# Turning the residual in blocks of 32 on VectorE and by small DMAs on POOL's queue

## The chip, the cores and the metric

The kernel runs on one core of one Trainium2 chip. The metric is the time of one execution on the device in microseconds (us). The profiler names the engines PE (TensorE, matmuls), PEld (its weight loads), DVE (VectorE), ACT (ScalarE), POOL (GpSimd) and SP (SyncE); SP, ACT and POOL can each issue DMAs on a queue of their own.

## What is computed

One layer of a decoder trunk over 512 tokens of width 1024, in float32. Cut to what matters here:

```
h   = rms_norm(x) ; z = h @ W_in                 # projections, gating, latent attention
x   = x + merged @ W_out                         # the residual x1
up  = conv3(rms_norm(x) @ w_up)                  # 2 x 2816 columns, causal depthwise conv, width 3
x   = x + (silu(gate) * val) @ w_down
out = rms_norm(x)                                # back to token-major rows
```

The end of the layer adds to x1 and takes a mean over the 1024 features of each token, so tokens must lie on the partitions there. Up to the up-projection the features lie on the partitions. Somewhere in between the residual x1 (512 tokens x 1024 features) has to be transposed.

## The kernel before

All matmuls run on float32 operands split in a high and a low part, three matmuls for one product (`mm3`, L79 to L82): `wsplit` lets ACT cast the high part (L70) and DVE subtract for the low part (L71).

**The residual.** `x1` is eight feature blocks j of 128 features x 512 tokens, in two tiles `x1_0` and `x1_1` of the pool hp (tags d0 and d1, L560). The same two buffers held vA before. The output projection adds to it on DVE (L571).

**The up-projection and the gated FFN** (the loop `for n in range(NF)`, 22 rounds): a round multiplies two column blocks of w_up (`pup`, 24 matmuls each), scales each by the broadcast row norm `r2` when it leaves PSUM (`conv`, `z = pup * r2`, L635), runs the convolution on ACT and DVE, and writes the product into `aT`. The last of these scalings in the program is that of block 43, `z43`. In rounds 4 to 11 `x1_turn(t, hf)` turns a piece of the residual: four PE transposes of 128x128 (L649) into a PSUM bank, and an ACT copy back into the same places of x1 (L650). In rounds 12 to 17 `fill` loads the first quarter of w_down, B11, into the six tiles `R` (L608, on SP's queue).

**The down-projection** is a scheme of seven products m1, m5, m6, m4, m3, m7, m2 (L689) of half-sized matrices; each is 11 blocks of 6 matmuls, and its right side comes in six pieces g = 0 to 5 of two blocks each (the last of one). A piece of `R` is split for the current product (`w_split`, L711), and right after that a DMA on POOL's queue adds the next quarter of w_down onto it in place (L606, `accum_op=add`), so that R[g] is the sum that the next product needs. m1 multiplies by B11 itself: its first matmul needs the cast of R[0]. For m3 the tile is loaded anew instead (L608, SP). `post`, `done` and `finish` add the products to the residual, take the squares, scale and store.

**Order and buffers.** A scheduler lays down each engine's instruction order when the program is built, by program order and priorities; each engine then works strictly in its order and waits on semaphores. A pool gives tiles of one tag the same buffers; a tile without a tag takes its name as its tag, within its pool. The pools hp and fp hold one buffer for each tag. The next tile of a tag gets the buffer when every instruction that reads or writes the earlier tile is done. Of the names below, fp holds these:

```
    r2 = fp.tile([P, S], F32, name="r2")
    aT = fp.tile([P, NF, S], F32, name="aT")
    R = [fp.tile([P, (hi - lo) * S], F32, name=f"r1_{lo}") for lo, hi in steps]
```

Of the kernel before, what the change touches and what calls it, by code (L numbers as in the profile page):

```python
# [7 lines left out]
F32 = mybir.dt.float32  # L8
# [3 lines left out]
AF = mybir.ActivationFunctionType  # L12
ALU = mybir.AluOpType
AX = mybir.AxisListType

P = 128
D = 1024
S = 512
NT = S // P
KC = D // P  # L20
# [3 lines left out]
NF = DFF // P  # L24
# [18 lines left out]
def block_kernel(ctx, tc, xT, pos, w_s, w_v, w_g, w_q, w_kv, w_o, w_u, w_d,  # L43
                 ws_t, bs, vg, vb, par, cst, fnl, out):
    nc = tc.nc
    V, A, T, G, SY = nc.vector, nc.scalar, nc.tensor, nc.gpsimd, nc.sync
# [3 lines left out]
    hp = ctx.enter_context(tc.tile_pool(name="hp", bufs=1))  # L50
    ps = ctx.enter_context(tc.tile_pool(name="ps", bufs=8, space=bass.MemoryType.PSUM))

    def bank(n):
        return ps.tile([P, 512], F32, tag="ps", name=n)
# [53 lines left out]
    ident = cstt[:, CI:CI + P]  # L108
# [66 lines left out]
    cqL = [mx.tile([P, S], F32R, name=f"cqL{i}") for i in range(2)]  # L175
    ckH = mx.tile([P, S], F32R, name="ckH")
    ckL = mx.tile([P, S], F32R, name="ckL")
    vA2 = [hp.tile([P, 2 * D], F32, tag=f"d{t}", name=f"vA{t}") for t in range(2)]
    vA = [vA2[t // 2][:, (t % 2) * D:(t % 2 + 1) * D] for t in range(NT)]

    with tc.tile_pool(name="st", bufs=2) as st:

# [22 lines left out]
        for j in range(KC):  # L205
# [7 lines left out]
            lo = half * S  # L213
# [157 lines left out]
    with tc.tile_pool(name="at", bufs=1) as at:  # L371
# [119 lines left out]
        for h in range(H):  # L491
# [30 lines left out]
            if h < NT:  # L522
                t = h
# [16 lines left out]
    with tc.tile_pool(name="mg", bufs=2) as mg:  # L540
        for h in range(H):
            zb = zbs[h] if h in zbs else gate("b", 2 * H + h)
            pm = bank(f"pm{h}")
            c = slice(h * P, (h + 1) * P)
            for n in range(NT):
                T.matmul(pm[:, n * P:(n + 1) * P], lhsT=vA[n][:, c], rhs=wst[:, h], start=True, stop=True)
            t2 = mg.tile([P, S], F32, tag="t2", name=f"t2{h}")
            V.tensor_tensor(out=t2.rearrange("p (n t) -> p n t", n=NT),
                            in0=pm.rearrange("p (n t) -> p n t", n=NT),
                            in1=bsb[:, h:h + 1].to_broadcast([P, NT, P]), op=ALU.add)  # L550
            V.tensor_tensor(out=t2, in0=uT[h], in1=t2, op=ALU.mult)
            zz = mg.tile([P, S], F32, tag="zz", name=f"zz{h}")
            V.tensor_tensor(out=zz, in0=zb, in1=yB[h], op=ALU.mult)
            V.tensor_tensor(out=zz, in0=zz, in1=t2, op=ALU.add)
            mH.append(uy.tile([P, S], F32R, tag=f"u{h}", name=f"mH{h}"))
            mL.append(uy.tile([P, S], F32R, tag=f"y{h}", name=f"mL{h}"))
            split(mH[h], mL[h], zz)


        x1t = [hp.tile([P, NT, NT, P], F32, tag=f"d{t}", name=f"x1_{t}") for t in range(2)]  # L560
        x1 = [x1t[j // NT][:, j % NT].rearrange("p t c -> p (t c)") for j in range(KC)]
        acc2 = hp.tile([P, S], F32, name="acc2")
        for j in range(KC):
            SY.dma_start(x1[j], xT[j])
            raw = wtile(w_o[j], f"o{j}")
            wh, wl = wsplit(raw, f"o{j}")
            po = bank(f"pout{j}")
            for h in range(H):
                c = slice(h * P, (h + 1) * P)
                mm3(po, wh[:, c], wl[:, c], mH[h], mL[h], h == 0, h == H - 1)  # L570
            V.tensor_tensor(out=x1[j], in0=po, in1=x1[j], op=ALU.add)  # L571
            htiles(j, "f")
            g_ = part[:, PFF + j:PFF + j + 1]
            A.mul(hH[j], x1[j], g_)
            V.scalar_tensor_tensor(out=hL[j], in0=x1[j], scalar=g_, in1=hH[j].bitcast(F32),
                                   op0=ALU.mult, op1=ALU.subtract)
            sq = acc2 if j == 0 else mg.tile([P, S], F32, tag="sq2", name=f"sq2_{j}")
            A.activation(out=sq, in_=x1[j], func=AF.Square)
            if j:
                V.tensor_tensor(out=acc2, in0=acc2, in1=sq, op=ALU.add)  # L580
# [14 lines left out]
    NS = len(steps)  # L595
    B11, B12, B21, B22 = (w_d[k, f] for k in range(2) for f in range(2))

    R = [fp.tile([P, (hi - lo) * S], F32, name=f"r1_{lo}") for lo, hi in steps]

    def cols(g):  # L600
        lo, hi = steps[g]
        return slice(lo * S, hi * S)

    def fill(q, g, add=True):
        if add:
            G.dma_start(R[g], q[:, cols(g)], accum_op=ALU.add)  # L606
        else:
            SY.dma_start(R[g], q[:, cols(g)])  # L608

    def a_sides(lo, hi):  # L610

# [30 lines left out]
                               op0=ALU.mult, op1=ALU.add)  # L642
        return y

    def x1_turn(t, hf):

        pt = bank(f"pt{t}{hf}")
        for q in range(NT):
            T.transpose(pt[:, q * P:(q + 1) * P], x1t[hf][:, q, t, :], ident)  # L649
        A.copy(x1t[hf][:, :, t, :], pt.rearrange("p (q c) -> p q c", q=NT))  # L650

    with tc.tile_pool(name="f2", bufs=2) as f2:
        for n in range(NF):
            i = n // 2 + (n % 2) * KH
            pg = up(2 * n)
            if n == 0:
                rt = rooted([acc2], 0, f2, "f")
                pv = up(1)
                A.copy(r2, over_partitions(rt, f2, "f"))
            yg = conv(pg, i)  # L660
            if n:
                pv = up(2 * n + 1)
            A.activation(out=yg, in_=yg, func=AF.Silu)  # L663
            yv = conv(pv, NF + i)
            V.tensor_tensor(out=aT[:, i], in0=yg, in1=yv, op=ALU.mult)
            if n % 4 == 3 or n == NF - 1:
                a_sides(n // 4 * 2, n // 2 + 1)
            if 4 <= n < 12:
                x1_turn((n - 4) // 2, n % 2)
            if 12 <= n < 12 + NS:  # L670
                fill(B11, n - 12, False)

# [43 lines left out]

    def res(t, f):

        return x1t[f][:, :, t, :]

    def b3(t):
        return t.rearrange("p (q c) -> p q c", q=NT)

    def plus(t, f, t_):
        V.tensor_tensor(out=res(t, f), in0=res(t, f), in1=b3(t_), op=ALU.add)

    def done(t, f, p_, op=ALU.add):
        V.tensor_tensor(out=res(t, f), in0=res(t, f), in1=b3(p_), op=op)  # L730
        j_ = dp.tile([P, S], F32, tag="j", name=f"j{t}{f}", bufs=2)
        A.activation(out=b3(j_), in_=res(t, f), func=AF.Square, accum_out=ms[:, t, f:f + 1])
        if f:
            V.tensor_tensor(out=res(t, f), in0=res(t, f), in1=b3(gfb[:, S:]), op=ALU.mult)

    def finish(t):

        V.tensor_scalar(out=ms[:, t, 2:3], in0=ms[:, t, 0:1], scalar1=ms[:, t, 1:2], scalar2=1.0 / D,
                        op0=ALU.add, op1=ALU.mult)
        V.tensor_scalar(out=ms[:, t, 2:3], in0=ms[:, t, 2:3], scalar1=EPS, scalar2=None, op0=ALU.add)  # L740
        G.tensor_tensor(out=ms[:, t, 3:4], in0=ms[:, t, 2:3], in1=mhalf[:, 0:1], op=ALU.pow)
        r_ = ms[:, t, 3:4]
        V.scalar_tensor_tensor(out=res(t, 0), in0=res(t, 0), scalar=r_, in1=b3(gfb[:, :S]),
                               op0=ALU.mult, op1=ALU.mult)
        A.mul(res(t, 1), res(t, 1), r_)
        SY.dma_start(out[t, :, :S], res(t, 0))
        A.dma_start(out[t, :, S:], res(t, 1))
# [143 lines left out]
```

## Time and profile before

| | us |
|---|---|
| median of 3 runs | 696.66 (696.41 to 697.33) |
| the profiled execution, its own time | 697.01 |
| span in its trace, first to last instruction | 695.3 |
| up-projection on PE, first to last matmul | about 336 to 581 |
| down-projection on PE, first matmul | 580.75 |

The page of the profile gives for each engine the busy time and its share of the span. A row of a timeline has the start in us, the duration in us, the engine, the line, the operation with its output and input tiles (without buffer numbers), the shapes and, in square brackets, the idle time of that engine ahead of it and what ended it. "POOLq" and "SPq" are the queues on which an engine issues DMAs; a DMA's time "to landing" runs from its issue to its completion. A row of PE times one matmul with its pipeline, so starts, not durations, tell the rate.

### The profile page before, as it was taken

The numbers are of one execution on the slowest core, as the hardware profiler recorded it, in microseconds if no ns is written. First come the engines' busy times: TensorE is split into PE (matmuls) and PEld (weight loads), VectorE is DVE, ScalarE is ACT, GpSimd is POOL, SyncE is SP. The second block draws the span as 40 slices with busy tenths as digits, with TensorE's granted clock in tenths as the row PEclk, the third lists the DMA queues.
The fourth block names the chain that finished last, engine by engine and source line by source line (L and its number), as shares of the span: only waits on it lengthen the run. The fifth ranks groups of instructions, "written<-read, shape, count | busy, mean of one in ns | idle before, by whom it ended". The sixth has DMA issues, their size and how long they took to land.

```text
span 695.3 us, 8489 instructions
## 1 busy us (share of the span) xinstructions
PE 684.6 (98%) x3183; PEld 569.4 (82%) x3183; DVE 522.6 (75%) x859; ACT 353.9 (51%) x519; POOL 36.0 (5%) x42
## 2 busy tenths in 40 slices
PE   9999999999999999999999999999999999999994
PEld 6888888888888888888888888888888888888883
DVE  7966699877768678855577868778677789579884
ACT  6465556775765552343354344444344335565672
POOL 0000110000000000000100000000000002330201
PEclk9999999999999999999999999999999999999998
DMA  8424522131120112353542222223322236997824
GB/s 269 153 78 139 186 84 83 61 115 31 61 88 34 62 61 91 109 177 107 180 170 90 92 91 90 92 90 99 114 91 91 91 91 118 197 187 202 159 76 122
DMA packets 28026, 78.67 MB, mean 113 GB/s; under 512 B 3024, under 2 KB 7632, under 8 KB 27984
## 3 DMA queue, kind: packets, MB, share of 16 engines
q1 hardware_dynamic: 21408, 62.92, 27.4%
q0 software_dynamic: 3456, 11.54, 9.3%
q10 hardware_dynamic: 3120, 3.67, 1.7%
q8 instruction: 25, 0.41, 0.2%
q14 instruction: 17, 0.14, 0.1%
HBM read 76.02 MB, written 2.10 MB: 112 GB/s over the span
## 4 chain that ended last, share of the span: by engine, by line
PE 96%; DVE 1%; issue 1%; POOL 0%; ACT 0%; POOLq 0%
PE pup L80 12%; PE pup L82 12%; PE pup L81 11%; PE m L82 4%; PE m L81 4%; PE m L80 4%; PE pout L81 2%; PE pv L80 2%; PE pout L80 2%; PE pza L81 2%; PE pza L80 2%; PE pzb L80 2%; PE pzb L82 2%; PE pzu L81 2%; PE pzb L81 2%; PE pv L82 2%
## 5 line engine op out<-in xcount | busy, mean ns | idle before, releaser
L70 ACT CAST wh_u<-wr_u 128x1024 fp32r<-128x1024 f32 x44 | 46.3, 1051 | 84.4 <-issue 49.6
L71 DVE TENSOR_TENSOR wl_u<-wr_u,wh_u 128x1024 fp32r<-128x1024 f32 x44 | 53.9, 1224 | 9.9 <-ACT wh_u L70 9.6
L635 DVE TENSOR_TENSOR z<-pup,r 128x512 f32<-128x512 f32 x44 | 30.3, 690 | 40.3 <-PE pup L82 40.3
L82 PE MATMUL m<-wh_m,al_m 128*128 128x512 f32 x132 | 51.5, 390 | 0.6 <-DVE al_m L77 0.6
L80 PE MATMUL m<-wh_m,ah_m 128*128 128x512 f32 x132 | 51.4, 389 | 0.0
L81 PE MATMUL m<-wl_m,ah_m 128*128 128x512 f32 x132 | 51.4, 389 | 0.0
L70 ACT CAST wh_g<-wr_g 128x1024 fp32r<-128x1024 f32 x24 | 25.2, 1049 | 49.4 <-issue 30.6
L71 DVE TENSOR_TENSOR wl_m<-r,wh_m 128x1024 fp32r<-128x1024 f32 (+1 forms) x36 | 40.7, 1131 | 6.3 <-ACT wh_m L70 6.3
L70 ACT CAST wh_m<-r 128x1024 fp32r<-128x1024 f32 (+1 forms) x36 | 35.3, 980 | 19.6 <-PE m L82 19.1
L637 ACT ACTIVATE y<-z,part 128x512 f32<-128x512 f32 x44 | 35.7, 814 | 2.6 <-DVE z L635 2.4
L663 ACT ACTIVATE y<-y 128x512 f32<-128x512 f32 x22 | 13.9, 633 | 45.0 <-DVE y L641 45.0
L606 POOL DMA_DIRECT2D r<-in_w_d_dram x24 | 21.4, 890 | 287.0 <-DVE wl_m L71 270.7
L71 DVE TENSOR_TENSOR wl_g<-wr_g,wh_g 128x1024 fp32r<-128x1024 f32 x24 | 29.4, 1223 | 7.2 <-ACT wh_g L70 7.1
L641 DVE SCALAR_TENSOR_TENSOR y<-z,part,y 128x512 f32<-128x512 f32 x44 | 33.0, 751 | 1.4
L639 DVE SCALAR_TENSOR_TENSOR y<-z,part,y 128x512 f32<-128x512 f32 x44 | 32.8, 747 | 0.7 <-ACT y L637 0.7
L82 PEld LDWEIGHTS m<-wh_m,al_m 128*128 128x128 f32 x132 | 24.8, 188 | 6.1 <-DVE al_m L77 1.0
L81 PEld LDWEIGHTS m<-wl_m,ah_m 128*128 128x128 f32 x132 | 24.8, 188 | 5.2
L80 PEld LDWEIGHTS m<-wh_m,ah_m 128*128 128x128 f32 x132 | 24.8, 188 | 5.2
L81 PE MATMUL pout<-mL,wh_o 128*128 128x512 f32 x64 | 25.3, 395 | 0.0
L80 PE MATMUL pout<-mH,wh_o 128*128 128x512 f32 x64 | 25.0, 394 | 0.0
L82 PE MATMUL pout<-mH,wl_o 128*128 128x512 f32 x64 | 24.9, 389 | 0.0
L77 DVE TENSOR_TENSOR al_m<-aT,ah_m 128x1024 fp32r<-128x1024 f32 (+1 forms) x12 | 13.6, 1134 | 11.9 <-ACT ah_m L76 11.9
(565 smaller groups left out, 2004.0 us busy)
## 6 DMA issues: line engine op xcount, KB each, us to landing
wr_u<-in_w_u_dram SPq DMA_DIRECT2D x44, 512.0 KB, 3.3
wr_g<-in_w_g_dram SPq DMA_DIRECT2D x24, 512.0 KB, 3.4
r<-in_w_d_dram POOLq DMA_DIRECT2D x20, 512.0 KB, 7.2
r<-in_w_d_dram SPq DMA_DIRECT2D x10, 512.0 KB, 6.1
x<-in_xT_dram SPq DMA_DIRECT2D x16, 256.0 KB, 4.5
wr_v<-in_w_v_dram SPq DMA_DIRECT2D x8, 512.0 KB, 4.1
wr_o<-in_w_o_dram SPq DMA_DIRECT2D x8, 512.0 KB, 3.2
wr_m<-in_w_d_dram SPq DMA_DIRECT2D x5, 512.0 KB, 3.5
```

Of the source, the lines that this page charges most:

```text
L70: A.copy(th[:, lo:hi], raw[:, lo:hi])
L71: V.tensor_tensor(out=tl[:, lo:hi], in0=raw[:, lo:hi], in1=th[:, lo:hi].bitcast(F32), op=ALU.subtract)
L77: V.tensor_tensor(out=tl, in0=src, in1=th.bitcast(F32), op=ALU.subtract)
L80: T.matmul(o, lhsT=wh, rhs=xh, start=start, stop=False)
L81: T.matmul(o, lhsT=wh, rhs=xl, start=False, stop=False)
L82: T.matmul(o, lhsT=wl, rhs=xh, start=False, stop=stop)
L606: G.dma_start(R[g], q[:, cols(g)], accum_op=ALU.add)
L635: V.tensor_tensor(out=z[:, 2:], in0=pz, in1=r2, op=ALU.mult)
L637: A.activation(out=y, in_=z[:, 2:], func=AF.Identity, scale=part[:, w + 2:w + 3], bias=part[:, PCB + f:PCB + f + 1])
L639: V.scalar_tensor_tensor(out=y, in0=z[:, 1:S + 1], scalar=part[:, w + 1:w + 2], in1=y, op0=ALU.mult, op1=ALU.add)
L641: V.scalar_tensor_tensor(out=y, in0=z[:, 0:S], scalar=part[:, w:w + 1], in1=y, op0=ALU.mult, op1=ALU.add)
L663: A.activation(out=yg, in_=yg, func=AF.Silu)
```

## The change

The residual's two tiles become one tile `x1` with tag d. In rounds 0 to 3 DVE transposes each block j into a tile `xq` by blocks of 32x32 (`squares`, L650 of the changed kernel); four tiles `xq0` to `xq3` hold two blocks each. They have the tags r0 to r3, which four of the six tiles `R` now have as well (tags r0 to r5), and a tile of `R` is made at its first `fill`. In rounds 4 to 19 `x1_turn(j, rows)` moves the 32x32 blocks to their places in a new tile `xt` (tag d too): 8 DMAs a round on POOL's queue, 128 in all, each of 32 partitions x 4 runs of 32 elements (128 bytes). All loads of `R` move from SP's queue to POOL's; B11 is loaded in the rounds 16 to 21. The PE transposes and their ACT copies go. The end of the kernel reads whole rows of `xt`.

```diff
--- before.py
+++ after.py
@@ -175,8 +175,8 @@
     cqL = [mx.tile([P, S], F32R, name=f"cqL{i}") for i in range(2)]
     ckH = mx.tile([P, S], F32R, name="ckH")
     ckL = mx.tile([P, S], F32R, name="ckL")
-    vA2 = [hp.tile([P, 2 * D], F32, tag=f"d{t}", name=f"vA{t}") for t in range(2)]
-    vA = [vA2[t // 2][:, (t % 2) * D:(t % 2 + 1) * D] for t in range(NT)]
+    vA4 = hp.tile([P, NT, D], F32, tag="d", name="vA")
+    vA = [vA4[:, t] for t in range(NT)]
 
     with tc.tile_pool(name="st", bufs=2) as st:
 
@@ -557,8 +557,8 @@
             split(mH[h], mL[h], zz)
 
 
-        x1t = [hp.tile([P, NT, NT, P], F32, tag=f"d{t}", name=f"x1_{t}") for t in range(2)]
-        x1 = [x1t[j // NT][:, j % NT].rearrange("p t c -> p (t c)") for j in range(KC)]
+        x1t = hp.tile([P, KC, S], F32, tag="d", name="x1")
+        x1 = [x1t[:, j] for j in range(KC)]
         acc2 = hp.tile([P, S], F32, name="acc2")
         for j in range(KC):
             SY.dma_start(x1[j], xT[j])
@@ -595,17 +595,21 @@
     NS = len(steps)
     B11, B12, B21, B22 = (w_d[k, f] for k in range(2) for f in range(2))
 
-    R = [fp.tile([P, (hi - lo) * S], F32, name=f"r1_{lo}") for lo, hi in steps]
+    xq = [fp.tile([P, D], F32, tag=f"r{q}", name=f"xq{q}") for q in range(KC // 2)]
+    R = [None] * NS
 
     def cols(g):
         lo, hi = steps[g]
         return slice(lo * S, hi * S)
 
     def fill(q, g, add=True):
+        if R[g] is None:
+            lo, hi = steps[g]
+            R[g] = fp.tile([P, (hi - lo) * S], F32, tag=f"r{g}", name=f"r1_{lo}")
         if add:
             G.dma_start(R[g], q[:, cols(g)], accum_op=ALU.add)
         else:
-            SY.dma_start(R[g], q[:, cols(g)])
+            G.dma_start(R[g], q[:, cols(g)])
 
     def a_sides(lo, hi):
 
@@ -642,12 +646,20 @@
                                op0=ALU.mult, op1=ALU.add)
         return y
 
-    def x1_turn(t, hf):
-
-        pt = bank(f"pt{t}{hf}")
-        for q in range(NT):
-            T.transpose(pt[:, q * P:(q + 1) * P], x1t[hf][:, q, t, :], ident)
-        A.copy(x1t[hf][:, :, t, :], pt.rearrange("p (q c) -> p q c", q=NT))
+    def squares(j):
+        V.transpose(out=xq[j // 2][:, (j % 2) * S:(j % 2 + 1) * S], in_=x1[j])
+
+    xt = []
+
+    def x1_turn(j, rows):
+
+        if not xt:
+            xt.append(hp.tile([P, NT, D], F32, tag="d", name="xt"))
+        q = xq[j // 2][:, (j % 2) * S:(j % 2 + 1) * S].rearrange("p (t c f) -> p t c f", t=NT, c=NT)
+        for a in rows:
+            for c in range(NT):
+                G.dma_start(xt[0][32 * c:32 * c + 32, :, j * P + 32 * a:j * P + 32 * a + 32],
+                            q[32 * a:32 * a + 32, :, c])
 
     with tc.tile_pool(name="f2", bufs=2) as f2:
         for n in range(NF):
@@ -665,10 +677,13 @@
             V.tensor_tensor(out=aT[:, i], in0=yg, in1=yv, op=ALU.mult)
             if n % 4 == 3 or n == NF - 1:
                 a_sides(n // 4 * 2, n // 2 + 1)
-            if 4 <= n < 12:
-                x1_turn((n - 4) // 2, n % 2)
-            if 12 <= n < 12 + NS:
-                fill(B11, n - 12, False)
+            if n < 4:
+                squares(2 * n)
+                squares(2 * n + 1)
+            elif n < 20:
+                x1_turn((n - 4) // 2, (0, 1) if n % 2 == 0 else (2, 3))
+            if n >= NF - NS:
+                fill(B11, (n - NF + NS + 4) % NS, False)
 
 
 
@@ -718,20 +733,17 @@
 
     def res(t, f):
 
-        return x1t[f][:, :, t, :]
-
-    def b3(t):
-        return t.rearrange("p (q c) -> p q c", q=NT)
+        return xt[0][:, t, f * S:(f + 1) * S]
 
     def plus(t, f, t_):
-        V.tensor_tensor(out=res(t, f), in0=res(t, f), in1=b3(t_), op=ALU.add)
+        V.tensor_tensor(out=res(t, f), in0=res(t, f), in1=t_, op=ALU.add)
 
     def done(t, f, p_, op=ALU.add):
-        V.tensor_tensor(out=res(t, f), in0=res(t, f), in1=b3(p_), op=op)
+        V.tensor_tensor(out=res(t, f), in0=res(t, f), in1=p_, op=op)
         j_ = dp.tile([P, S], F32, tag="j", name=f"j{t}{f}", bufs=2)
-        A.activation(out=b3(j_), in_=res(t, f), func=AF.Square, accum_out=ms[:, t, f:f + 1])
+        A.activation(out=j_, in_=res(t, f), func=AF.Square, accum_out=ms[:, t, f:f + 1])
         if f:
-            V.tensor_tensor(out=res(t, f), in0=res(t, f), in1=b3(gfb[:, S:]), op=ALU.mult)
+            V.tensor_tensor(out=res(t, f), in0=res(t, f), in1=gfb[:, S:], op=ALU.mult)
 
     def finish(t):
 
@@ -740,7 +752,7 @@
         V.tensor_scalar(out=ms[:, t, 2:3], in0=ms[:, t, 2:3], scalar1=EPS, scalar2=None, op0=ALU.add)
         G.tensor_tensor(out=ms[:, t, 3:4], in0=ms[:, t, 2:3], in1=mhalf[:, 0:1], op=ALU.pow)
         r_ = ms[:, t, 3:4]
-        V.scalar_tensor_tensor(out=res(t, 0), in0=res(t, 0), scalar=r_, in1=b3(gfb[:, :S]),
+        V.scalar_tensor_tensor(out=res(t, 0), in0=res(t, 0), scalar=r_, in1=gfb[:, :S],
                                op0=ALU.mult, op1=ALU.mult)
         A.mul(res(t, 1), res(t, 1), r_)
         SY.dma_start(out[t, :, :S], res(t, 0))
```

How this stands in the built program, at three places. In the names below, `m10` to `m15` are the six pieces of m1, `m50` and on those of m5, and `wl_` and `wh_` are the parts of a split weight.

The first place is DVE's order at the end of the up-projection, before, from the split of m5's left side (`al_m54`) on:

```order
L77 TENSOR_TENSOR al_m54_4980<-s1_3088,ah_m54_4979 128x1024
L635 TENSOR_TENSOR z43_4916<-pup43_4890,r2_3086 128x512
L71 TENSOR_TENSOR wl_m12_4952<-r1_4_3094,wh_m12_4951 128x1024
L639 SCALAR_TENSOR_TENSOR y43_4917<-z43_4916,part_67,y43_4917 128x512
L641 SCALAR_TENSOR_TENSOR y43_4917<-z43_4916,part_67,y43_4917 128x512
L71 TENSOR_TENSOR wl_m13_4975<-r1_6_3095,wh_m13_4974 128x1024
L665 TENSOR_TENSOR aT_3087<-y21_4878,y43_4917 128x512
L616 TENSOR_TENSOR s1_3088<-aT_3087 128x256
```

and the same stretch in the changed kernel, from the last scaling by r2 (`z43`) on:

```order
L639 TENSOR_TENSOR z43_5005<-pup43_4979,r2_3084 128x512
L650 STREAM_TRANSPOSE xq2_3092<-x1_2764 128x512 x2
L643 SCALAR_TENSOR_TENSOR y43_5006<-z43_5005,part_67,y43_5006 128x512
L645 SCALAR_TENSOR_TENSOR y43_5006<-z43_5005,part_67,y43_5006 128x512
L677 TENSOR_TENSOR aT_3085<-y21_4967,y43_5006 128x512
L620 TENSOR_TENSOR s1_3086<-aT_3085 128x256
L621 TENSOR_TENSOR aT_3085<-aT_3085 128x256
L622 TENSOR_TENSOR aT_3085<-s1_3086,aT_3085 128x256
L623 TENSOR_TENSOR s4_3087<-aT_3085 128x256
L77 TENSOR_TENSOR al_m58_5092<-s1_3086,ah_m58_5091 128x768
L71 TENSOR_TENSOR wl_m10_5033<-r1_0_4759,wh_m10_5032 128x1024
L71 TENSOR_TENSOR wl_m11_5038<-r1_2_4853,wh_m11_5037 128x1024
```

The two transposes into `xq2` stand behind `z43`, all other transposes far ahead of it; the splits of m1's pieces have moved from among the convolution to behind it.

The second place is POOL's order from the attention's last instruction (`rv3`) on, before (`rt_f` is the row norm of the FFN, the DMAs add to the tiles of `R`):

```order
L531 TENSOR_TENSOR rv3_1723<-rv3_1723,mhalf_84 128x1
L147 TENSOR_TENSOR rt_f_3138<-ms_f_3137,mhalf_84 128x4
L606 DMA r1_0_3092<-in_w_d_dram 128x1024
L606 DMA r1_2_3093<-in_w_d_dram 128x1024
L606 DMA r1_4_3094<-in_w_d_dram 128x1024
L606 DMA r1_6_3095<-in_w_d_dram 128x1024
L606 DMA r1_8_3096<-in_w_d_dram 128x1024
L606 DMA r1_10_3097<-in_w_d_dram 128x512
```

and in the changed kernel, from the next instruction on:

```order
L612 DMA r1_8_4583<-in_w_d_dram 128x1024
L612 DMA r1_10_4671<-in_w_d_dram 128x512
L147 TENSOR_TENSOR rt_f_3134<-ms_f_3133,mhalf_84 128x4
L661 DMA xt_3524<-xq0_3090 32x4x32 x32
L661 DMA xt_3524<-xq1_3091 32x4x32 x32
L661 DMA xt_3524<-xq2_3092 32x4x32 x32
L661 DMA xt_3524<-xq3_3093 32x4x32 x24
L612 DMA r1_0_4759<-in_w_d_dram 128x1024
L661 DMA xt_3524<-xq3_3093 32x4x32 x8
L612 DMA r1_2_4853<-in_w_d_dram 128x1024
L612 DMA r1_4_4933<-in_w_d_dram 128x1024
L612 DMA r1_6_5019<-in_w_d_dram 128x1024
```

Two loads of `R` (pieces 4 and 5) now stand ahead of `rt_f`; behind it come 120 small DMAs, then the load of R[0], 8 more small DMAs, and the loads of R[1] to R[3].

The third place is DVE's order at the start of the up-projection in the changed kernel, from the last sum of squares (`acc2`) on; before, the rows with STREAM_TRANSPOSE are not there and the rest stands in the same order:

```order
L580 TENSOR_TENSOR acc2_2765<-acc2_2765,sq2_7_3073 128x512
L650 STREAM_TRANSPOSE xq0_3090<-x1_2764 128x512 x2
L650 STREAM_TRANSPOSE xq1_3091<-x1_2764 128x512 x2
L146 TENSOR_SCALAR ms_f_3133<-pm_f_3128 128x4
L650 STREAM_TRANSPOSE xq3_3093<-x1_2764 128x512
L71 TENSOR_TENSOR wl_u3_3241<-wr_u3_3238,wh_u3_3240 128x1024
L134 SCALAR_TENSOR_TENSOR dL_f_3169<-cstt_69,rt_f_3134,dH_f_3168 128x128 x4
L650 STREAM_TRANSPOSE xq3_3093<-x1_2764 128x512
L71 TENSOR_TENSOR wl_u4_3283<-wr_u4_3280,wh_u4_3282 128x1024
```

Four transposes have come ahead of `ms_f`, from which `rt_f` is computed, and two behind it.

## Rows read from the trace of the kernel before

**Rows 1.** The page: busy us (share of the span) and instructions of each engine.
```profile
PE 684.6 (98%) x3183; PEld 569.4 (82%) x3183; DVE 522.6 (75%) x859; ACT 353.9 (51%) x519; POOL 36.0 (5%) x42
```

**Rows 2.** Stretches: us, PE, PEld, DVE, ACT, POOL busy (instructions), clock, DMA share, GB/s.
```profile
560.00:580.00 20.00, 20.00 (x90) 16.57 (x89) 17.43 (x26) 9.01 (x12) 1.94 (x2) 1.00 0.38 82
580.00:596.00 16.00, 16.00 (x73) 13.23 (x72) 12.47 (x17) 8.36 (x11) 3.96 (x5) 1.00 0.83 157
596.00:680.00 84.00, 84.00 (x372) 69.49 (x371) 67.90 (x77) 51.33 (x65) 17.54 (x20) 1.00 0.77 163
680.00:696.00 16.00, 5.96 (x25) 4.26 (x24) 5.75 (x11) 4.12 (x8) 1.32 (x3) 0.81 0.37 102
```

**Rows 3.** Instructions on tile pt: duration in ns (min/median/max), first and last start.
```profile
L649 PE MATMUL pt<-cstt,x x32: 270/272/273, 391.9 to 471.8; 128*128 128x128 f32 x32
L650 ACT COPY x<-pt x8: 575/582/583, 392.9 to 472.4; 128x512 f32<-128x512 f32 x8
```

**Rows 4.** Chain of waits, 385 to 420: start, us, what.
```profile
392.08 0.44 PE pt L649 x4
```

**Rows 5.** Timeline of PE, 579.9 to 581.5.
```profile
580.52 0.39 PE L82 MATMUL pup<-h7f,wl_u 128*128 128x512 f32 x1
580.75 0.39 PE L80 MATMUL m<-wh_m,a1h 128*128 128x512 f32 x1
```

**Rows 6.** Timeline of PE, 595 to 596.5.
```profile
595.48 0.39 PE L82 MATMUL m<-wh_m,a1l 128*128 128x512 f32 x1
595.71 0.39 PE L80 MATMUL m<-wh_m,ah_m 128*128 128x512 f32 x1
```

**Rows 7.** Timeline of DVE, 574 to 584.
```profile
576.42 1.23 DVE L71 TENSOR_TENSOR wl_m<-r,wh_m 128x1024 fp32r<-128x1024 f32 x1 [0.22 <-ACT wh_m L70]
...
580.55 1.22 DVE L77 TENSOR_TENSOR al_m<-s,ah_m 128x1024 fp32r<-128x1024 f32 x1
581.69 0.68 DVE L635 TENSOR_TENSOR z<-pup,r 128x512 f32<-128x512 f32 x1
```

**Rows 8.** Instructions on the tiles of R and on r2.
```profile
L70 ACT CAST wh_m<-r x36: 624/1052/1057, 569.9 to 663.9; 128x1024 fp32r<-128x1024 f32 x30, 128x512 fp32r<-128x512 f32 x6
L71 DVE TENSOR_TENSOR wl_m<-r,wh_m x36: 683/1218/1226, 571.0 to 664.6; 128x1024 fp32r<-128x1024 f32 x30, 128x512 fp32r<-128x512 f32 x6
L606 POOL DMA_DIRECT2D r<-in_w_d_dram x24: 875/881/1063, 572.5 to 652.1; - x24
L608 SPq DMA_DIRECT2D r<-in_w_d_dram x12: 327/328/437, 339.7 to 636.1; - x12
```

**Rows 9.** Line 606, the DMAs on POOL's queue: time to landing.
```profile
DMA to landing us min/median/max: 5.6/7.2/8.9
```

**Rows 10.** Line 608, the loads on SP's queue: time to landing.
```profile
DMA to landing us min/median/max: 3.7/5.2/7.5
```

**Rows 11.** Timeline of POOL, 610 to 618.
```profile
614.12 0.88 POOL L606 DMA_DIRECT2D r<-in_w_d_dram  x1 [2.72 <-DVE wl_m L71]
615.41 0.88 POOL L606 DMA_DIRECT2D r<-in_w_d_dram  x1 [0.41 <-issue]
```

**Rows 12.** Timeline of SP's queue, 339 to 352.
```profile
339.69 1.28 SPq L608 DMA_DIRECT2D r<-in_w_d_dram  x3
```

**Rows 13.** The page: DMA queue, kind: packets, MB, share of 16 engines.
```profile
q1 hardware_dynamic: 21408, 62.92, 27.4%
q0 software_dynamic: 3456, 11.54, 9.3%
q10 hardware_dynamic: 3120, 3.67, 1.7%
```

**Rows 14.** Timeline of DVE, 338.5 to 346.
```profile
342.48 0.16 DVE L146 TENSOR_SCALAR ms_f<-pm_f 128x4 f32<-128x4 f32 x1 [2.88 <-PE pm_f L120]
```

**Rows 15.** Timeline of PE, 0 to 8.
```profile
1.29 4.02 PE L114 MATMUL warm<-wz 128*128 128x512 bf16 x9 [1.29 <-DVE wz L96]
...
7.41 0.40 PE L82 MATMUL pS<-h0a,wl_s 128*128 128x512 f32 x1
```

## The prediction

> **What bounds the kernel now.** I read the page's busy times first, then a table of stretches, then the timelines around the seam between up-projection and down-projection. PE is busy 684.6 us of the span of 695.3 [rows 1], and in every stretch up to 680 us it is busy without a gap at granted clock 1.00, the higher of its two levels, 2.4 GHz [rows 2]. The seam is closed too: the last up-projection matmul starts at 580.52, the first of m1 at 580.75 [rows 5]. So whatever PE no longer has to do is gained, and whatever PE must newly wait for at the seam is lost in full. POOL has 36.0 us of work in the whole span [rows 1] and hardly any ahead of the seam; that idle engine is what the change uses. The question is when it may begin.
>
> **What goes from PE.** A turn of four transposes takes 0.44 us on the chain [rows 4], and there are eight turns (32 transposes, eight ACT copies [rows 3]): 8 x 0.44 = 3.5 us, all on the path, since PE is full. The ACT copies lay beside it and give nothing.
>
> **What is added at the start.** Four transposes on DVE now stand ahead of `ms_f`, which waits for PE's `pm_f`; DVE sat idle 2.88 us there [rows 14]. The trace of before has no transpose on DVE. From below it is 0.43 us, from above I take double the 0.68 of `z` [rows 7], the nearest row of the same size, 128x512 in float32; I take 0.69. 4 x 0.69 = 2.76 fits the idle time. At the upper end (5.4 us) the row norm would be some 2.6 us late, and part of that PE's. I take 0. The two loads ahead of `rt_f` on POOL take 2 x 0.88 [rows 8] and end in the same idle time.
>
> **Where the new wait is.** The tile `xq2` has the tag r2. In the same pool the row norm's tile has no tag and is called r2, so its tag is r2 as well, with one buffer. `xq2` gets it only when the last reader of the row norm is done, and that is `z43`, the last scaling of the up-projection. DVE's order shows just that: two transposes into `xq2` directly behind `z43`. That alone would hold back 32 DMAs. But `xt` takes the buffer (tag d) of `x1`, and these two transposes are the last readers of `x1`. So the very first of the 128 DMAs waits for them, though `xq0` and `xq1` have been ready since the start of the up-projection. And on POOL's queue the load of R[0], without which m1 cannot begin, stands behind 120 of the 128; the loads of R[1] to R[3] behind all of them. PE has nothing else: m1 is next in its order. The up-projection's 230 us, which could have covered the DMAs, are over when they begin.
>
> **The sum.** In the trace's time of before, less 3.5:
> - The last up-projection matmul starts at 580.52 and lasts 0.39 [rows 5]: it ends at 577.4. `z43` began at 581.69 before, behind a split of 1.22 at 580.55, and with a split of 1.23 of m1's weights ahead of both [rows 7] that now comes later. So I let it start 0.1 after the matmul, at 577.5, and end at 578.2. Two transposes: 579.6.
> - One small DMA on POOL. Each has 32 x 4 = 128 pieces, as many as a load of R has rows, and loads of R take POOL 0.88 us each (24 of them, 875 ns to 1063 [rows 8]), whether the rows are of 4 or of 2 KB. The closest pair of them starts 1.29 apart [rows 11]. SP's queue, which has three in a row with 0.33 each, takes 1.28 for the three [rows 8, 12], so some 0.1 lies between two. Between 0.98 and 1.29 I take 1.05, nearer to the first, since the pair on POOL may hold a wait.
> - 120 x 1.05 = 126.0: the load of R[0] is issued at 705.6. A load of R took 5.2 us to land on SP's queue (3.7 to 7.5 [rows 10]) and an addition 7.2 on POOL's (5.6 to 8.9 [rows 9]). I take 6.0, then the cast of 1.05 [rows 8]: PE starts m1 at about 712.7 and does 12 of its 66 matmuls.
> - R[1] is issued 9 x 1.05 later, at 715.1, lands at 721.1, is cast at 722.1 and split 1.22 later [rows 8], at 723.4. R[2] and R[3] follow 1.05 apart and land ahead of PE. m1 took 595.71 - 580.75 = 14.96 us for 66 matmuls [rows 5, 6], 0.227 each; the last 52 take 11.8 and end at 735.2.
> - Before, m5 began at 595.71, now at 735.2: 139.5 us later. From there on PE's work and the order of the additions are those of before, and the first addition is issued about 23 us ahead of its use before [rows 6, 8] and some 17 now, against a landing of 8.9 at most. I take no loss.
> - Storing whole rows of 2 KB from `xt` may save a few tenths at the end; I leave it at 0.
>
> Span 695.3 + 139.5 = 834.8; the execution's own time was 697.01, 1.7 above its span, so 836.5. That execution lies 0.35 above the median of its runs: 836.
>
> **What the cost of a small DMA may be.** Each 0.1 us is worth 129 x 0.1 = 12.9 us here. At 0.88 the time is 814, at 1.29 it is 867. Two other limits: from the ninth on, each DMA waits for the one eight places ahead of it to land; at 2.9 to 8.9 us to landing for an eighth each that is 0.4 to 1.1, no more than the issue. And the DMA engines: 144 packets for one small DMA (the 3456 of the additions, over 24 [rows 8, 13]) over 16 engines are 9 each; a packet took 61 ns on q10, 142 on q1 and 299 on q0 (share x 16 x 695.3 over the packets [rows 13]): 0.5, 1.3 or 2.7 us for one DMA. Packets of 128 bytes are far smaller than those of any of the three, so I lean to the first. The ends that I keep are 0.43, SP's pitch, and 2.7.
>
> The Trainium skill, "DMA: Bandwidth & Descriptors" (Rules for kernel authors), says that many small transfers should be coalesced, since one under 64 KB is mostly overhead. Its fit for one DMA on this path (Anatomy of one DMA) is about 2.0 us plus bytes over 436 GB/s; for 16 KB, an estimate from that page, 2.04 us, and with eight on the way 0.26 for each, by which the sum would end at 734. The rows on POOL's own 0.88 for each stand against that.
>
> **Rivals.**
> 1. *Small DMAs dearer than any load of R*, because the writing of three-dimensional patterns or the packets' engines are slower: d from 1.29 to 2.7, the time 867 to 1049; at twice a load's 0.88, 928. For it: the pattern is not in the trace. Against it: the same number of pieces and a seventh of the bytes or less.
> 2. *Cheaper ones*, since a plain copy is not an addition: from 0.43 to 0.88, the time 756 to 814. Against it: no POOL DMA took under 875 ns [rows 8].
> 3. *Not slower.* If the order of the wait were another and POOL began when the transposes into `xq3` are done, at about 347, it would have up to the seam, 230 us, for 128 DMAs. Up to 1.8 us each they would all be hidden, and the change gives back PE's 3.5 us: 693. It decides at 1.8. For it: POOL's idleness [rows 1]. Against it: DVE's order, which cannot be passed.
> 4. *PE comes back slow and stays so.* After the long idle stretch its pace could be that of the start, where nine matmuls of the same width took 4.02 us, 0.447 each; by 7.4 us it has its full pace [rows 15]. For the first 12 of m1 this is hidden, since R[1] is awaited anyway. If the rest of the down-projection (some 440 matmuls) ran at 0.447, it would be 97 us more: 933.
>
> In rival 3 the skill's page "SBUF — State Buffer" (SBUF: two separate sides) adds a caution: POOL cannot write descriptors while certain DVE operations hold a shared port. No row here shows it, and where I expect the DMAs DVE is idle.
>
> **How the numbers follow.** Forecast 0.62 (its own range 814 to 867), rival 1 0.20, rival 2 0.11, rival 3 0.03, rival 4 0.04. The range of 8 in 10 takes in all of the forecast's and the near parts of rivals 1 and 2: 800 to 900. A measurement of this kernel can tell about 0.2% from no change. Slower by more: all but rival 3, 0.97; rival 3 is split, faster 0.02, same 0.01.
>
> **What would show it.** PE idle from about 577 to 712, with a short burst and a second gap to 722, then full; POOL in 128 close rows that begin right behind two STREAM_TRANSPOSE rows and `z43`; their pitch gives d. The up-projection ends 3.5 us earlier with no gap near 348. The prediction is wrong in its mechanism if the first small DMA starts anywhere in the up-projection, and in its size if the pitch is outside 0.88 to 1.29.

## The result, and the profile after

The changed kernel takes 773.82 us (773.71 to 774.65, 4 runs) against 696.59 (696.41 to 697.33) of the kernel before on the same chip: 1.1107 times as long, 95% interval 1.1094 to 1.1121, 77.2 us more. The direction, the wait and its cause are as forecast; the size is not: 836 was forecast, with 800 to 900 as the range. The profiled execution has a span of 772.0 us and took 773.71.

The page's busy times, which answer to [rows 1]:

```profile
PE 683.8 (89%) x3151; PEld 567.2 (73%) x3151; DVE 527.0 (68%) x867; ACT 350.5 (45%) x511; POOL 112.0 (15%) x182
```

PE's busy time is nearly the same (683.8 us for 684.6: 32 matmuls fewer, and the first of m1 slower, as seen below); POOL has 76 us more. What the kernel lost is then idle time of PE, and the table of stretches, with the columns of [rows 2], shows where it lies:

```profile
577.00:654.00 77.00, 0.00 (x0) 0.00 (x0) 6.42 (x11) 2.26 (x3) 70.48 (x128) 0.51 0.20 41
654.00:657.00 3.00, 2.48 (x5) 1.56 (x6) 1.23 (x1) 0.43 (x1) 2.21 (x5) 0.50 0.32 46
657.00:660.00 3.00, 3.00 (x8) 2.32 (x8) 0.29 (x1) 1.04 (x1) 1.16 (x2) 0.50 1.07 365
660.00:663.00 3.00, 3.00 (x12) 2.10 (x12) 1.33 (x2) 1.24 (x2) 0.89 (x1) 0.91 0.98 220
663.00:666.00 3.00, 2.88 (x13) 2.05 (x12) 2.94 (x3) 1.80 (x2) 1.33 (x2) 1.00 1.07 210
```

For 77 us PE does nothing and POOL issues its 128 small DMAs, with the DMA engines a fifth busy. Then PE works again, six microseconds of it at a granted clock of 0.50, the lower of its two levels (1.2 GHz). What releases the small DMAs is in DVE's timeline at the seam, the answer to [rows 7]:

```profile
576.78 0.69 DVE L639 TENSOR_TENSOR z<-pup,r 128x512 f32<-128x512 f32 x1
577.50 1.30 DVE L650 STREAM_TRANSPOSE xq<-x 128x512 f32<-128x512 f32 x2
```

`z43` (L639 now) is followed at once by the two transposes into `xq2`, and POOL's timeline starts behind them:

```profile
579.11 6.06 POOL L661 DMA_DIRECT2D xt<-xq  x11 [236.27 <-DVE xq L650]
585.49 12.77 POOL L661 DMA_DIRECT2D xt<-xq  x22 [0.33 <-issue]
598.64 50.57 POOL L661 DMA_DIRECT2D xt<-xq  x87 [0.39 <-issue]
649.26 0.58 POOL L612 DMA_DIRECT2D r<-in_w_d_dram  x1
...
654.85 1.23 POOL L612 DMA_DIRECT2D r<-in_w_d_dram  x2
```

120 small DMAs stand ahead of the load of R[0] (L612, at 649.26): 70.15 us, 0.585 each. The instructions by line, with the duration in ns (min/median/max); the small DMAs first, with the three stops of POOL among them ("issue": us, times):

```profile
L661 POOL DMA_DIRECT2D xt<-xq x128: 551/551/617, 579.1 to 654.3; - x128
...
  issue: 1.1, 3
...
DMA to landing us min/median/max: 1.6/1.7/3.8
```

then the plain loads of `R`, which before were on SP's queue [rows 8, 10]:

```profile
L612 POOL DMA_DIRECT2D r<-in_w_d_dram x12: 540/560/741, 339.4 to 714.1; - x12
...
DMA to landing us min/median/max: 3.8/4.1/6.7
```

and the additions, the same operation as in [rows 8]:

```profile
L610 POOL DMA_DIRECT2D r<-in_w_d_dram x24: 851/870/930, 657.3 to 729.1; - x24
```

The additions cost POOL 870 ns, about as before (881). A plain DMA costs less on the same queue: 551 ns with 128 pieces of 128 bytes, 560 with 128 rows of up to 4 KB.

The other side of the wait is PE's timeline. The second column is the duration of the group, starts give the pace:

```profile
575.71 0.39 PE L82 MATMUL pup<-h7f,wl_u 128*128 128x512 f32 x1
654.48 1.22 PE L80 MATMUL m<-wh_m,a1h 128*128 128x512 f32 x2 [78.38 <-ACT wh_m L70]
...
657.19 0.63 PE L82 MATMUL m<-wh_m,a1l 128*128 128x512 f32 x1
657.62 0.63 PE L80 MATMUL m<-wh_m,a1h 128*128 128x512 f32 x1
...
660.18 0.81 PE L80 MATMUL m<-wh_m,a1h 128*128 128x512 f32 x2
660.99 0.50 PE L81 MATMUL m<-wl_m,a1h 128*128 128x512 f32 x1
661.33 0.40 PE L82 MATMUL m<-wh_m,a1l 128*128 128x512 f32 x1
661.56 0.39 PE L81 MATMUL m<-wl_m,a1h 128*128 128x512 f32 x1
...
673.35 0.39 PE L80 MATMUL m<-wh_m,ah_m 128*128 128x512 f32 x1
```

The last matmul of the up-projection starts at 575.71, the first of m1 at 654.48, the first of m5 at 673.35. Matmuls start 0.43 apart up to 660.2 (657.19 to 657.62) and 0.23 apart from 661.33 on. At the start of the up-projection DVE's timeline, to be compared with [rows 14], has the four added transposes:

```profile
338.69 2.49 DVE L650 STREAM_TRANSPOSE xq<-x 128x512 f32<-128x512 f32 x4
341.55 0.16 DVE L146 TENSOR_SCALAR ms_f<-pm_f 128x4 f32<-128x4 f32 x1 [0.36 <-PE pm_f L120]
```

The four take 2.49 us, and `ms_f` still waits 0.36 for PE.

The ledger of the span, before to after, by starts of matmuls [rows 5, 6 and the timelines of both kernels]: the up-projection's first starts at 336.05, now at 335.11 (-0.95); from there to its last it is 244.5 us, now 240.6 (-3.9); from that to the first of m1 it is 0.23, now 78.77 (+78.5); m1 takes 14.96, now 18.87 (+3.9); from m5's first matmul, at 673.35 now, to the end of the span it is 99.6, now 98.65 (-0.9). The sum is +76.7, which is the difference of the spans. The first term is no effect of the change: in the traces of experiments 1 and 3 to 7, which do the same work up to there, the up-projection starts anywhere from 335.51 to 336.50.

### The profile page after: what moved, and what is told of

Read it like the earlier page. It is cut to its first block, busy times and chain, and to the rows that moved or that the text cites. A ratio compares the mean times of both kernels' runs of the same rounds, so it can differ in the third digit from the quotient of the medians.

```text
span 772.0 us, 8567 instructions
## 1 busy us (share of the span) xinstructions
PE 683.8 (89%) x3151; PEld 567.2 (73%) x3151; DVE 527.0 (68%) x867; ACT 350.5 (45%) x511; POOL 112.0 (15%) x182
## 3 DMA queue, kind: packets, MB, share of 16 engines
q0 software_dynamic: 9152, 19.41, 11.9%
## 4 chain that ended last, share of the span: by engine, by line
PE 85%; POOL 10%; DVE 2%; issue 2%; DMA 1%; ACT 0%; POOLq 0%; ACTq 0%
PE pup L80 10%; PE pup L82 10%; PE pup L81 10%; POOL xt L661 9%; PE m L82 4%; PE m L81 4%; PE m L80 4%; PE pout L81 2%; PE pv L80 2%; PE pout L80 2%; PE pza L81 2%; PE pza L80 2%; PE pzb L80 2%; PE pzb L82 2%; PE pzu L81 2%; PE pzb L81 2%
## 5 line engine op out<-in xcount | busy, mean ns | idle before, releaser
L661 POOL DMA_DIRECT2D xt<-xq x128 | 70.7, 553 | 240.7 <-DVE xq L650 236.3
L80 PE MATMUL m<-wh_m,a1h 128*128 128x512 f32 x22 | 9.5, 449 | 78.4 <-ACT wh_m L70 78.4
L80 PEld LDWEIGHTS m<-wh_m,a1h 128*128 128x128 f32 x22 | 4.8, 225 | 79.8 <-ACT wh_m L70 78.8
L639 DVE TENSOR_TENSOR z<-pup,r 128x512 f32<-128x512 f32 x44 | 30.3, 690 | 38.0 <-PE pup L82 38.0
L612 POOL DMA_DIRECT2D r<-in_w_d_dram x12 | 6.9, 573 | 234.5 <-DVE acc L580 224.2
L610 POOL DMA_DIRECT2D r<-in_w_d_dram x24 | 21.0, 874 | 39.0 <-DVE wl_m L71 25.3
```

The lines of the kernel that those rows point to most:

```text
L80: T.matmul(o, lhsT=wh, rhs=xh, start=start, stop=False)
L639: V.tensor_tensor(out=z[:, 2:], in0=pz, in1=r2, op=ALU.mult)
L661: G.dma_start(xt[0][32 * c:32 * c + 32, :, j * P + 32 * a:j * P + 32 * a + 32], q[32 * a:32 * a + 32, :, c])
```

## The experiments

Theory throughout: the shared tag ties the small DMAs to `z43`, and their issue on POOL, one price for each, sets the length of the gap. The experiments test the tie (1, 2), the price (3 to 5, 8) and the place of R's loads on the queue (6, 7). The kernel before ran beside all of them on the same chips, at 696.75 (experiments 1 to 4) and 696.84 (5 to 8).

**1. The row norm in a buffer of its own.**

```diff
-    r2 = fp.tile([P, S], F32, name="r2")
+    r2 = fp.tile([P, S], F32, tag="rn", name="r2")
```

> Only edit: the row norm's tile r2 gets a tag of its own, so xq2 no longer shares its buffer. Theory (the shared tag r2 held the last two transposes, and through them all 128 DMAs, behind the last scaling z43): the first small DMA starts near 346 us, right behind the transposes into xq3; 128 at 0.58 us end near 421, 155 us ahead of the seam; PE has no gap at the seam. Time: 696.6, less 3.9 that the up-projection was shorter in the changed kernel (241.0 against 244.9 us), less 1.0 by which it began earlier, less 0.9 from m5 on: 691. Rival (the DMAs themselves, of 128-byte pieces, cost the time wherever they stand, by crowding the loads of w_up or POOL's queue): PE waits appear in the up-projection, time above 700.

Measured: 691.76 us (691.73 to 693.9, 5 runs), 0.9935 times the kernel before (0.9917 to 0.9953). POOL's timeline, with all 128 small DMAs (the last at 423.0) inside the up-projection:

```profile
347.08 14.12 POOL L661 DMA_DIRECT2D xt<-xq  x25 [3.80 <-DVE xq L650]
...
```

and what PE waited for in the whole execution (us in total, times, longest):

```profile
PE warm L114 <- DVE wz L96: 1.3, 1, 1.3
PE m L82 <- DVE al_m L77: 0.6, 1, 0.6
```

One word in a tile's declaration is worth 82 us. With the tie gone the changed kernel is also 0.65% faster than the kernel before, a small gain, but outside the interval. The 5.3 us by which its span is shorter than before are 4.4 up to the start of m1 (580.75 to 576.38; 3.8 of them lie within the up-projection) and 0.9 behind m5. The DMAs ran beside a busy DVE here, as the stretch from 345 to 430 shows:

```profile
345.00:430.00 85.00, 85.00 (x377) 70.33 (x376) 64.57 (x99) 35.96 (x44) 72.64 (x132) 1.00 0.50 144
```

and the durations of line 661:

```profile
L661 POOL DMA_DIRECT2D xt<-xq x128: 548/548/617, 347.1 to 423.0; - x128
...
DMA to landing us min/median/max: 1.6/2.4/4.5
```

DVE is busy 64.6 of 85 us, and the issue takes as long as beside an idle DVE (548 for 551 ns, 617 at most in both); the landing takes 2.4 us instead of 1.7. The caution of the Trainium skill that the prediction named under rival 3 ("SBUF — State Buffer", SBUF: two separate sides) is therefore not seen with the operations that DVE runs here.

**2. The tie left, x1 and xt in two tiles by feature halves.** If the DMAs of `xq0` and `xq1` wait only because `xt` is one tile in the buffer of one `x1`, these 64 must go free. The diff shows the main lines; `vA`, which has the same buffers, becomes two tiles again, and the places that index the halves follow.

```diff
-        x1t = hp.tile([P, KC, S], F32, tag="d", name="x1")
-        x1 = [x1t[:, j] for j in range(KC)]
+        x1t = [hp.tile([P, NT, S], F32, tag=f"d{t}", name=f"x1_{t}") for t in range(2)]
+        x1 = [x1t[j // NT][:, j % NT] for j in range(KC)]
...
-        if not xt:
-            xt.append(hp.tile([P, NT, D], F32, tag="d", name="xt"))
+        f = j // NT
+        if len(xt) == f:
+            xt.append(hp.tile([P, NT, S], F32, tag=f"d{f}", name=f"xt{f}"))
```

> The shared tag r2 stays; x1 and xt are two tiles each, by halves of the features, so that the first half of xt waits only for the transposes into xq0 and xq1. Theory of two steps (the tag holds xq2, and x1's single buffer carries that hold to the other 64 DMAs): 64 DMAs start near 342 and end near 380, the other 64 behind z43 near 579; the load of R[2] comes 64 x 0.585 = 37.4 us later, at 616.5, lands at 620.6; PE idles from about 582 to 622 and m5 starts near 635 instead of 673: 773.8 - 38 = 736. Rival (the hold of xq2 alone stops POOL's queue, or the pitch is set by something that piles up with time): all 128 behind z43, 774; or half the DMAs at another pitch, a time off by more than 6.

Measured: 735.48 us (734.54 to 737.69), ratio 1.0557 (1.0536 to 1.0578). POOL's timeline at the seam:

```profile
580.16 5.73 POOL L662 DMA_DIRECT2D xt<-xq  x10 [5.16 <-DVE xq L650]
586.35 31.38 POOL L662 DMA_DIRECT2D xt<-xq  x54 [0.46 <-issue]
```

and PE's waits:

```profile
PE m L80 <- ACT wh_m L70: 40.2, 1, 40.2
```

64 DMAs ran between 342.3 and 381, the other 64 behind the transposes into `xq2`; PE's wait falls from 78.4 to 40.2. Both links are shown: the tag r2 holds `xq2`, and the buffer of `x1` passes the hold on to what does not need `xq2`.

**3. Half as many DMAs of twice the size.** The same bytes in the same 128-byte pieces: 64 DMAs of 256 pieces. The transposes write `xq` in another order for it (pieces of 128x128), and the readers of `xt` follow. In the last line of the diff, `o` and `q` are views of `xt` and `xq` in the new order.

```diff
-        V.transpose(out=xq[j // 2][:, (j % 2) * S:(j % 2 + 1) * S], in_=x1[j])
+        o = xq[j // 2].rearrange("p (t u c) -> p t u c", t=NT, u=2)
+        for t in range(NT):
+            V.transpose(out=o[:, t, j % 2], in_=x1[j][:, t * P:(t + 1) * P])
...
-                G.dma_start(xt[0][32 * c:32 * c + 32, :, j * P + 32 * a:j * P + 32 * a + 32],
-                            q[32 * a:32 * a + 32, :, c])
+                G.dma_start(o[32 * c:32 * c + 32, :, a], q[32 * a:32 * a + 32, :, c])
```

> The shared tag stays; xt is laid out by pairs of feature blocks, so that 64 DMAs of 32 partitions x 8 runs of 128 bytes replace the 128 of 4 runs. Theory A (POOL's time for a DMA is in proportion to its pieces): about 1.1 us each, 60 of them ahead of R[0] take 66 us, time 770. Theory B (a fixed cost for each DMA): 0.585 us each, 35 us, time 739. Theory C (part and part): between them; the pitch minus 0.585 over 128 is the price of a piece.

Measured: 749.68 us (749.01 to 749.96), ratio 1.0755 (1.0738 to 1.0771), between a cost for each piece (770) and one for each DMA (739). POOL's timeline:

```profile
580.85 1.84 POOL L664 DMA_DIRECT2D xt<-xq  x3 [236.63 <-DVE xq L652]
583.15 1.75 POOL L664 DMA_DIRECT2D xt<-xq  x3 [0.47 <-issue]
...
626.09 0.59 POOL L612 DMA_DIRECT2D r<-in_w_d_dram  x1
```

and the durations:

```profile
L664 POOL DMA_DIRECT2D xt<-xq x64: 582/582/662, 580.8 to 630.7; - x64
```

The issue itself grew only from 551 to 582 ns for twice the pieces. But after three DMAs or fewer POOL stops, "issue" by the profile: 21 times ahead of the load of R[0], once for 2.2 us and otherwise for 0.16 to 0.47, 8.6 us in all. So it is (626.09 - 580.85) / 60 = 0.754 for each. The kernel with 128 pieces has such stops only three times in its 128 (1.1 us in all).

**4. Twice as many DMAs of half the size.**

```diff
-                G.dma_start(xt[0][32 * c:32 * c + 32, :, j * P + 32 * a:j * P + 32 * a + 32],
-                            q[32 * a:32 * a + 32, :, c])
+                for u in (slice(0, 2), slice(2, 4)):
+                    G.dma_start(xt[0][32 * c:32 * c + 32, u, j * P + 32 * a:j * P + 32 * a + 32],
+                                q[32 * a:32 * a + 32, u, c])
```

> The shared tag stays; each small DMA is cut in two of 32 partitions x 2 runs, 256 in all, the same bytes. Theory A (in proportion to the pieces): 0.29 us each, 240 ahead of R[0] take 70 us, time 774. Theory B (fixed cost): 0.585 each, 140 us, time 844. Theory C: between, and on one line with the runs of 128 and 256 pieces.

Measured: 836.08 us (835.19 to 837.34), ratio 1.1997 (1.1976 to 1.2018).

```profile
579.62 126.30 POOL L662 DMA_DIRECT2D xt<-xq  x240 [236.27 <-DVE xq L650]
705.91 0.58 POOL L612 DMA_DIRECT2D r<-in_w_d_dram  x1
```

and the durations:

```profile
L662 POOL DMA_DIRECT2D xt<-xq x256: 533/533/608, 579.6 to 714.4; - x128
```

240 DMAs of 64 pieces in 126.3 us, 0.526 each, without a stop. So the price hangs on the number of DMAs and hardly on the pieces: 0.533, 0.551 and 0.582 us of issue for 64, 128 and 256 pieces. The Trainium skill, "DMA: Bandwidth & Descriptors" (Anatomy of one DMA), says that many descriptors can be emitted before an added cost shows; these three numbers agree. The time is 8 us under theory B's 844: 240 DMAs at 0.526 for 0.585 are 14 us less, but R[1] stands behind 16 DMAs here, and PE waits once more behind its first 12 matmuls:

```profile
720.01 1.22 PE L80 MATMUL m<-wh_m,a1h 128*128 128x512 f32 x2 [4.07 <-ACT wh_m L70]
```

**5. Experiment 3 with twice the scratch for DMAs.** If the stops of experiment 3 come from a full store in which POOL prepares its DMAs, a larger one ends them.

```diff
-    nc = bacc.Bacc("TRN2", target_bir_lowering=False, num_devices=1, dynamic_dma_scratch_size=1024)
+    nc = bacc.Bacc("TRN2", target_bir_lowering=False, num_devices=1, dynamic_dma_scratch_size=2048)
```

> The kernel of e3 (64 DMAs of 256 pieces behind z43) with twice the room that the program sets aside for descriptors of POOL's DMAs (2048 in place of 1024). In e3 one issue took 0.582 us but they came 0.754 apart, in threes with gaps of 0.3 to 0.5. Theory (POOL waits for room for the next descriptors): the gaps go, pitch near 0.61, the 60 ahead of R[0] take 36.5 us in place of 45.2, time 749.7 - 8.7 = 741. Rival (the wait for the landing of the one eight ahead, or the DMA engines at this many pieces): pitch stays at 0.75, time 750.

Measured: 739.39 us (738.74 to 739.94), ratio 1.0611 (1.0597 to 1.0626).

```profile
580.00 5.85 POOL L664 DMA_DIRECT2D xt<-xq  x10 [236.63 <-DVE xq L652]
586.40 13.38 POOL L664 DMA_DIRECT2D xt<-xq  x23 [0.54 <-issue]
600.14 15.71 POOL L664 DMA_DIRECT2D xt<-xq  x27 [0.36 <-issue]
615.86 0.59 POOL L612 DMA_DIRECT2D r<-in_w_d_dram  x1
```

Two stops are left, and the pitch is (615.86 - 580.00) / 60 = 0.598. That the size of this scratch set the stops is shown, and without them the time is the 739 that a price for each DMA gave for experiment 3. Why POOL stops, a full store, is argued from the size alone.

**6. Experiment 1 with R's plain loads on SP's queue.**

```diff
-            G.dma_start(R[g], q[:, cols(g)])
+            SY.dma_start(R[g], q[:, cols(g)])
```

> The kernel of e1 (own tag) with the plain loads of R back on SP's queue. Theory (with the DMAs beside the up-projection, the queue of these loads is off the path): 691.8, within 0.7 of e1. Rival (POOL's queue with 128 DMAs, 30 sums and 12 loads costs something in the down-projection too): 689 to 690.5; or SP's loads of w_up are held up by the loads of R that wait for xq: PE waits appear, above 693.

Measured: 692.15 us (691.73 to 692.8, 5 runs), ratio 0.9935 (0.9922 to 0.9949), as experiment 1 within the spread of the two. With the tie gone it does not matter which queue loads `R`.

**7. The changed kernel with R's plain loads on SP's queue,** the edit of experiment 6 alone. If R[0] came late only because it stands behind 120 DMAs in a queue, this would free it.

> The changed kernel with the plain loads of R back on SP's queue, the shared tag r2 left in. Theory (the loads are held by the buffers of xq and the sums by POOL's queue, so the place of R[0] behind 120 DMAs is only the first of several holds): R[0] is loaded after 32 DMAs, near 599.5, R[1] near 618, R[2] near 637, but R[3] shares xq3's buffer and still waits for all 128, landing near 660; m5 starts near 670 instead of 673, time 770. Rival (the place of R's loads on POOL's queue makes the stall): near 700.

Measured: 776.42 us (774.58 to 776.6), ratio 1.1137 (1.1122 to 1.1152): no gain over the 773.82 of the changed kernel. PE's timeline at its four restarts:

```profile
605.86 1.22 PE L80 MATMUL m<-wh_m,a1h 128*128 128x512 f32 x2 [28.79 <-ACT wh_m L70]
...
624.90 1.22 PE L80 MATMUL m<-wh_m,a1h 128*128 128x512 f32 x2 [14.01 <-ACT wh_m L70]
...
644.00 1.22 PE L80 MATMUL m<-wh_m,a1h 128*128 128x512 f32 x2 [13.40 <-ACT wh_m L70]
...
665.41 1.22 PE L80 MATMUL m<-wh_m,a1h 128*128 128x512 f32 x2 [16.66 <-ACT wh_m L70]
```

R[0] to R[3] take the buffers of `xq0` to `xq3`, and each is free only when the 32 DMAs that read it are through: 32 x 0.585 = 18.7, and the restarts lie 19.0, 19.1 and 21.4 apart. PE idles 72.9 us in four parts instead of 78.4 in one, but each time it comes back at the slow pace (the pair of 1.22 us), and m5 starts at 675.3 instead of 673.35. So the place in POOL's queue cost R[0] 48.6 us (654.48 - 605.86), but R[3], whose buffer the last 32 DMAs read, is as late as before. The expectation (770) was 6 us short. Its parts were not tested apart; three are in the trace: the DMAs start at 580.6 instead of 579.11, 1.0 of it because the whole up-projection lies that much later in this trace; R[3] is cast 6 us after its load's issue, beside additions, where 4.2 is this run's median landing; and the last 30 matmuls of m1 take 9.8 us (665.41 to 675.25) behind the slow restart, where 30 x 0.227 is 6.8.

**8. The kernel before, its additions replaced by plain loads** (the sums are left out).

```diff
-            G.dma_start(R[g], q[:, cols(g)], accum_op=ALU.add)
+            G.dma_start(R[g], q[:, cols(g)])
```

> The kernel before, with the DMAs that add to R turned into plain loads of the same blocks, so the sums of w_down are left out. Theory (the addition makes POOL's issue take 0.88; a plain DMA of 128 rows takes 0.56): 0.55 to 0.57 each in the same places, time unchanged at 697 within 1. Rival (what goes on beside it, full DMA engines and a busy DVE, makes it 0.88): stays near 0.88.

Measured, one run: 696.78 us.

```profile
L606 POOL DMA_DIRECT2D r<-in_w_d_dram x24: 537/540/718, 572.3 to 650.5; - x24
...
DMA to landing us min/median/max: 3.1/3.9/4.9
```

The same 24 DMAs at the same places cost POOL 540 ns instead of 881 and land after 3.9 us instead of 7.2 [rows 8, 9]. The 0.88 from which the prediction worked was the price of an addition. The time did not move; in the profile of the kernel before no engine waits for these DMAs.

## Why the prediction came out wrong in size

- *Where the wait is and why*: right. Experiments 1 and 2 show both links, the tag and the buffer of `x1`; the forecast start of POOL, 579.6, came out as 579.11. That it came so close is in part luck: the last matmul of the up-projection started 1.3 us earlier than forecast (575.71 for 577.0), and `z43` 1.07 behind it, where 0.5 was taken. That R[0] waits in POOL's queue is right too, but experiment 7 shows that the buffer of `xq3` would have held R[3] nearly as long; the prediction did not name this second hold.
- *The price of one small DMA*: the step that failed. Forecast 1.05, measured 0.585, for 120 of them 55.8 us of the 62.8 by which the forecast execution was too long. It was put together from 0.88, called the price of "loads of R", and a gap up to 1.29. All 24 rows on POOL's queue were additions (L606, `accum_op`); the loads of R (L608) were on SP's. The row gave the price of another operation, and experiment 8 shows that the addition alone makes the difference: 0.88 falls to 0.54. The pair 1.29 apart seems to have held a wait, as the prediction half suspected: the small DMAs follow each other after 0.03, and in the trace after, where an addition follows another 1.28 later (at 665.54), the profile names a wait of 0.42 for `wl_m` between them. The count of packets was off too, without effect on the 1.05: experiment 4 has 128 more small DMAs and on POOL's queue 13248 packets for 9152, 32 for each DMA and not 144.
- *Rival 2*, "a plain copy is not an addition", 0.43 to 0.88 and 756 to 814 us, is what happened, and it got 0.11. The argument against it, "no POOL DMA took under 875 ns", rested on rows of additions alone, so it did not bear on a plain copy. With 0.585 in place of 1.05 the prediction's own sum gives 836 - 129 x 0.465 = 776.
- *From R[0]'s issue to m5*: 29.6 forecast, 24.1 measured, 5.5 of the miss. Eight DMAs and the load of R[1] follow in 5.6 us, not 9.5, and a plain load has landed by 4.1 us where 6.0 was taken, a value between SP's landing and the additions'.
- *The smaller terms*: without the eight turns of PE the up-projection is 3.9 us shorter, where 3.5 was forecast; the four transposes at the start took 0.62 each (0.69 forecast) and cost nothing, as taken. The up-projection started 0.95 us earlier and the end of the layer took 0.9 less, both forecast as 0. The first is a difference between executions (see the ledger). The second lies behind the last scaling, where whole rows are stored now and not pieces of 512 bytes: from its start to the end of the span it is 4.7 us for 5.7, and the stores land after 2.9 us at most for 3.8; experiment 1 has the 0.9 as well. ACT also issues such a store in 0.37 us for 0.47, but that is not what counts: in experiment 3, with half rows, it is 0.47 still, and the end takes 4.6.

*PE at its restart.* The prediction held that a slow pace would be hidden for the first 12 matmuls, since R[1] is awaited anyway. ACT's casts of R[0] and R[1]:

```profile
653.39 1.04 ACT L70 CAST wh_m<-r 128x1024 fp32r<-128x1024 f32 x1 [71.05 <-DMA r<-in_w_d_dram]
658.63 1.04 ACT L70 CAST wh_m<-r 128x1024 fp32r<-128x1024 f32 x1 [4.20 <-DMA r<-in_w_d_dram]
```

and DVE's split of R[1]:

```profile
659.71 1.23 DVE L71 TENSOR_TENSOR wl_m<-r,wh_m 128x1024 fp32r<-128x1024 f32 x1 [4.02 <-ACT wh_m L70]
```

R[1] is split by 660.94, and the first matmul that needs the split starts at 660.99, right behind the 12 slow ones and the two on the cast. So the 12 were hidden, and the second gap that was forecast did not appear only because PE filled it at half pace (in experiment 4, where R[1] came later, a gap of 4.07 us is there): 3.0 of the 3.9 us by which m1 is longer are this wait. The 54 matmuls from R[1]'s cast on took 673.35 - 660.18 = 13.2 us, 0.9 more than at 0.227 each; more than that the lower clock did not cost. Rival 4's lasting slowness did not happen: from 661.3 on the pace is that of before.

## What to carry to other kernels

A tile that takes a buffer by name or tag also takes its last reader's place in time; before adding a tag, list the tiles that already have it, and follow each held tile on to the buffers that its own readers hold. Price an operation from rows of the same operation: an addition by DMA and a plain DMA on one queue look alike in a list and differ by 0.34 us, which 128 of them make 44. And where one queue feeds the next stage, moving the urgent load to another queue helps only if its buffer is free too.

## What the runs showed of the hardware beyond that

- A DMA issued by POOL costs it a nearly fixed time here: 0.53 to 0.58 us for 64 to 256 pieces of 128 bytes, 0.54 to 0.56 for 128 rows of up to 4 KB, and 0.87 to 0.88 when it adds.
- The DMA scratch of the program sets a second limit: DMAs of 256 pieces left POOL every 0.754 us with 1024 and every 0.598 with 2048.
- After 78 us without work PE came back at a granted clock of 0.50 (654 to 660), then 0.91 (660 to 663) and 1.00; after idle stretches of 13 to 29 us (experiment 7), and even of 4.07 us behind a burst of 12 matmuls (experiment 4), its first two matmuls were as slow, 1.22 us for the pair.
- Small DMAs land later in the midst of the up-projection (2.4 us in experiment 1, with the DMA engines half busy and DVE at work) than at the seam (1.7, a fifth busy), but are issued no slower. Which of the two, traffic or DVE, delays the landing was not tested.
